# Gate and up tiles of three feed-forward stages as 2x2 block products with seven multiplications in place of eight

## The chip, the cores and the metric

The kernel runs as one program on one core of a Trainium2 chip. The metric is the device time of one execution in microseconds; the median of the runs shown stands for the kernel. A profiled execution gives the trace, from which all durations here are read. Engines: PE is TensorE (matrix products), PEld its weight loads, DVE is VectorE, ACT is ScalarE, POOL is GpSimd, SP issues the DMAs.

## What is computed

Two layers of feed-forward, token mixing, feed-forward, for 512 positions of width 1024, hidden width 2816, all in f32:

```python
def modulate(h, shift, scale):
    return h * (1 + scale) + shift

def swiglu(h, wi, wo):
    gate, up = jnp.split(h @ wi, 2, axis=-1)
    return (jax.nn.silu(gate) * up) @ wo
...
    for l in range(DEPTH):
        mod = (c_act @ ada_w[l] + ada_b[l]).reshape(b, N_MOD, 1, D_MODEL)
        ...
        h = modulate(rmsnorm(x, norm_ffn1[l]), sh1, sc1)
        x = x + 0.5 * g1 * swiglu(h, ffn1_wi[l], ffn1_wo[l])
        h = modulate(rmsnorm(x, norm_mix[l]), sh2, sc2)
        x = x + g2 * token_mixing(h, cos, sin, w_in[l], sink[l], onorm_a[l], onorm_b[l], w_out[l])
        h = modulate(rmsnorm(x, norm_ffn2[l]), sh3, sc3)
        x = x + 0.5 * g3 * swiglu(h, ffn2_wi[l], ffn2_wo[l])
    return rmsnorm(x, final_norm)
```

## The kernel before

Activations lie transposed: 8 tiles of 128 features by 512 positions. Every f32 operand is split into a high part that TensorE takes in one pass (type F32R) and a low rest, and a product is three matmuls: high by high, low weight by high, high weight by low (`mm3`, lines 153 to 155). The weights come from HBM as raw f32 pieces of 128x1024 and are split on the chip by `emit_chunk`: ScalarE copies the high part (line 134), VectorE subtracts it (line 135). Buffers: two for `raw`, six each for `hi` and `lo`; `ahead` keeps three pieces emitted beyond the one in use.

A feed-forward stage (`ffn`) works in three parts of 7, 7 and 8 hidden tiles (THIRDS). For each hidden tile there are a gate tile and an up tile, each 8 x 3 matmuls of 512 columns into one PSUM bank; `take` then makes the product: Silu on ScalarE (line 362), times up on VectorE (363), and the split into `gh` and `gl` (367, 368). At the end of a part `out_tiles` multiplies these by the second weight, 8 output tiles of 7 or 8 x 3 matmuls, and adds the result to x (line 306). The first four tiles of a stage (`group`) are computed in two halves of 256 positions, since the normalised input of the second half is not there yet: `Norm.make` (lines 221 to 224) writes it in `hh` and `hl`, from a row statistic that comes by way of `stat` and `bcast`. The last four output tiles of a stage are done in halves as well.

There are four such stages: layer 0 first and second, layer 1 first and second; the first is started in another way (`start`). Between them lie the two mixers. Beside all this VectorE makes the modulation vectors: `ada_col` loads a piece of `ada_w` and multiplies it by `cs` with a sum (line 240), a step after each tile of the first stage (56 columns after the first 16) and of layer 0's second feed-forward stage (72 columns, with `cs` made anew by `ada_open`, matmuls of line 271).

The order of instructions on each engine is set by a scheduler from the program's order, priorities and buffer releases; each engine then runs its own queue strictly in that order. Pools decide how far anything can run ahead.

## Time and profile before

| | us |
|---|---|
| median of three runs | 1985.97 (1984.81 to 1990.3) |
| profiled execution, own time | 1988.23 |
| its span | 1986.2 |
| PE busy in it | 1955.2 (98%) |
| DVE busy | 1171.7 (59%) |
| ACT busy | 751.0 (38%) |
| granted TensorE clock, mean | 0.995 |

Busy time is the sum of an engine's instruction intervals; the intervals of matmuls overlap, so the pace of TensorE is read from the starts of its instructions. The same holds on VectorE: an instruction may start while the one before it is still listed.

### The profile page before, as it was taken

The page shows a single profiled execution, that of the slowest core. Times are in us where ns is not written, and L with a number is a line of the kernel's source. Part 1 is how long each engine was busy: PE and PEld are TensorE (multiplying, and loading weights), DVE is VectorE, ACT ScalarE, POOL GpSimd, SP SyncE. Part 2 cuts the span into 40 slices and gives each one's busy share as a digit, 9 for nine tenths or more (in the row PEclk, how much of TensorE's full clock was granted, in tenths as well). Part 3 has the DMA queues.
Part 4 walks back from the last instruction along what each step waited for, and adds up shares of the span by engine and source line. Part 5 has one row for each costly group of instructions (what it writes and reads, how often), then busy time and mean ns, then how long its engine had stood idle before and what let it go on. Part 6 is the DMA issues. An engine that isn't in the chain of part 4 may idle for free.

```text
span 1986.2 us, 25905 instructions
## 1 busy us (share of the span) xinstructions
PE 1955.2 (98%) x10016; PEld 1655.4 (83%) x10016; DVE 1171.7 (59%) x2131; ACT 751.0 (38%) x1332; POOL 92.7 (5%) x69
## 2 busy tenths in 40 slices
PE   6999999999999999999999999999999999999998
PEld 5888888998778888888898888889877898888888
DVE  7988433576798898733463333337678983333333
ACT  4422222345685422222242222223556752222223
POOL 4000000011210000000000000000121000000000
PEclk8999999999999999999999999999999999999999
DMA  7789433234412698733332333331544123333331
GB/s 255 272 309 337 129 101 101 84 108 118 127 44 94 222 335 322 248 105 98 94 96 85 106 90 102 97 104 58 155 107 106 54 75 98 104 98 95 104 96 43
DMA packets 84941, 266.96 MB, mean 134 GB/s; under 512 B 10706, under 2 KB 13906, under 8 KB 84820
## 3 DMA queue, kind: packets, MB, share of 16 engines
q1 hardware_dynamic: 84820, 265.33, 41.7%
q8 instruction: 78, 1.28, 0.3%
q14 instruction: 43, 0.35, 0.1%
HBM read 244.31 MB, written 2.10 MB: 124 GB/s over the span
## 4 chain that ended last, share of the span: by engine, by line
PE 89%; DVE 4%; DMA 2%; issue 2%; ACT 1%; POOL 0%; SPq 0%; DVEq 0%; ACTq 0%; POOLq 0%
PE mm L155 26%; PE mm L153 26%; PE mm L154 26%; PE ptr L516 2%; PE po L523 1%; PE po L524 1%; PE s L486 1%; PE s L487 1%; DVE lo L135 1%; PE mm L455 1%; PE mm L457 1%; PE mm L456 1%; PE p L531 1%; DVE araw L240 1%; DMA raw<-in_wo_dram 0%
## 5 line engine op out<-in xcount | busy, mean ns | idle before, releaser
L153 PE MATMUL mm<-hh,hi 128*128 128x512 f32 (+1 forms) x1776 | 662.3, 374 | 7.7 <-ACT hh L223 7.7
L155 PE MATMUL mm<-hl,hi 128*128 128x512 f32 (+1 forms) x1776 | 659.4, 373 | 2.0 <-DVE hl L224 2.0
L154 PE MATMUL mm<-hh,lo 128*128 128x512 f32 (+1 forms) x1776 | 661.4, 373 | 0.0
L134 ACT ACTIVATE hi<-raw 128x1024 fp32r<-128x1024 f32 (+5 forms) x365 | 335.0, 927 | 662.4 <-PE mm L155 575.1
L135 DVE TENSOR_TENSOR lo<-raw,hi 128x1024 fp32r<-128x1024 f32 (+5 forms) x365 | 397.1, 1094 | 311.4 <-ACT hi L134 309.1
L153 PEld LDWEIGHTS mm<-hh,hi 128*128 128x128 f32 x1776 | 336.2, 189 | 66.4 <-ACT hh L223 9.4
L155 PEld LDWEIGHTS mm<-hl,hi 128*128 128x128 f32 x1776 | 335.6, 189 | 60.6 <-DVE hl L224 3.2
L154 PEld LDWEIGHTS mm<-hh,lo 128*128 128x128 f32 x1776 | 335.9, 189 | 56.9
L154 PE MATMUL mm<-gh,lo 128*128 128x512 f32 (+1 forms) x832 | 296.9, 357 | 0.0
L155 PE MATMUL mm<-gl,hi 128*128 128x512 f32 (+1 forms) x832 | 296.6, 356 | 0.2 <-DVE gl L368 0.2
L153 PE MATMUL mm<-gh,hi 128*128 128x512 f32 (+1 forms) x832 | 296.7, 357 | 0.0
L306 DVE SCALAR_TENSOR_TENSOR x<-mm,fin,x 128x512 f32<-128x512 f32 (+1 forms) x156 | 101.9, 654 | 196.3 <-PE mm L155 195.7
L240 DVE CUSTOM_DVE_ANT_0 araw<-araw,cs 128x1024 f32<-128x1024 f32 x136 | 166.7, 1237 | 26.9 <-DMA araw<-in_adaT_dram 26.1
L155 PEld LDWEIGHTS mm<-gl,hi 128*128 128x128 f32 x832 | 157.2, 189 | 23.1 <-DVE gl L368 0.6
L154 PEld LDWEIGHTS mm<-gh,lo 128*128 128x128 f32 x832 | 157.2, 189 | 22.6
L153 PEld LDWEIGHTS mm<-gh,hi 128*128 128x128 f32 x832 | 157.2, 189 | 22.5
L362 ACT ACTIVATE sg<-mm 128x512 f32<-128x512 f32 x88 | 52.5, 598 | 283.7 <-PE mm L155 281.3
L363 DVE TENSOR_TENSOR sg<-sg,mm 128x512 f32<-128x512 f32 x88 | 60.4, 687 | 158.9 <-PE mm L155 157.4
L408 POOL TENSOR_TENSOR part<-part,rs 128x512 f32<-128x512 f32 x26 | 34.5, 1326 | 1274.2 <-DVE part L406 1272.0
L495 ACT ACTIVATE sm<-sm,nb 128x512 f32<-128x512 f32 (+2 forms) x128 | 81.6, 638 | 30.8 <-DVE nb L491 30.8
L516 PE MATMUL ptr<-ident,sm 128*128 128x128 f32 x416 | 81.5, 274 | 0.9 <-DVE pl L520 0.9
L520 DVE TENSOR_TENSOR pl<-ptr,ph 128x512 fp32r<-128x512 f32 (+2 forms) x128 | 73.2, 584 | 8.4 <-ACT ph L519 7.4
(142 smaller groups left out, 1793.2 us busy)
## 6 DMA issues: line engine op xcount, KB each, us to landing
raw<-in_wi_dram SPq DMA_DIRECT2D x170, 512.0 KB, 3.5
araw<-in_adaT_dram SPq DMA_DIRECT2D x144, 512.0 KB, 5.4
raw<-in_wo_dram SPq DMA_DIRECT2D x64, 448.0 KB, 3.4
raw<-in_wo_dram SPq DMA_DIRECT2D x32, 512.0 KB, 3.5
raw<-in_wqk_dram SPq DMA_DIRECT2D x26, 512.0 KB, 3.5
raw<-in_w_out_dram SPq DMA_DIRECT2D x16, 512.0 KB, 3.5
kh<-qh SPq DMA_DIRECT2D x40, 128.0 KB, 2.3
kl<-t SPq DMA_DIRECT2D x40, 128.0 KB, 2.3
```

Source lines behind the costliest of these rows:

```text
L134: A.activation(hi[:, sl], raw[:, sl], AF.Copy)
L135: V.tensor_tensor(lo[:, sl], raw[:, sl], hi.bitcast(F32)[:, sl], op=ALU.subtract)
L153: T.matmul(ps, wh, X[0][:, s], start=start, stop=False)
L154: T.matmul(ps, wl, X[0][:, s], start=False, stop=False)
L155: T.matmul(ps, wh, X[1][:, s], start=False, stop=stop)
L240: return V.tensor_tensor_reduce(out=raw, in0=raw, in1=ada["cs"], scale=1.0, scalar=0.0, op0=ALU.mult, op1=ALU.add, accum_out=mod[:, l, ch, ...
L306: V.scalar_tensor_tensor(x[:, m, s], ps[:, s], gate[:, m:m + 1], x[:, m, s], op0=ALU.mult, op1=ALU.add)
L362: A.activation(sg, pg, AF.Silu)
L363: V.tensor_tensor(sg, sg, pu, op=ALU.mult)
L495: A.activation(s[:, :w], s[:, :w], AF.Exp, scale=-1.0, bias=self.nb[:, qt:qt + 1], accum_out=self.den[:, qt:qt + 1])
L516: T.transpose(p[:, j * 128:j * 128 + 128], self.sm[qt][:, c0:c0 + 128], ident)
L520: V.tensor_tensor(pl[:, :w], p[:, :w], ph.bitcast(F32)[:, :w], op=ALU.subtract)
```

## The change

In three of the four feed-forward stages (all but the first) the gate and up tile of one hidden tile become one 2x2 block product. Rows of blocks are the two halves of the positions (256 each), columns are gate and up, and the inner dimension of 1024 is cut in two halves of 4 feature tiles. Seven products, each 4 x 3 matmuls of 256 columns, replace the eight blocks that 48 matmuls of 512 columns stand for. The first three hidden tiles of a stage (PLAIN) stay as they were; 19 tiles in each of the three stages are done in the new way (`pair`).

The seven products need sums of blocks. Those of the activations are made once in a stage (`sums`: four tiles of 4x256, split in `sh`, `sl`). Those of the weights are made for each hidden tile on the chip (`emit_pair`): from the raw gate and up pieces VectorE makes five 512-column differences and sums (lines 180, 182, 187, 189 and the split of the fourth), and three and a half pieces are split into high and low in place of two. The results lie in two PSUM banks whose halves are used by turns; ScalarE copies three intermediate halves out (lines 479, 487, 490) and VectorE adds them (493, 496, 498), Silu works in place (499), and the product and its split are taken one tile later (506 to 510).

With it go changes of buffers and order: `raw` has four buffers; `cs` is kept, so the second `ada_open` is gone; the 72 columns of layer 1 are spread over three stages (16 in the first, 32 in layer 0's second, 24 in layer 1's first), there with one `araw` buffer; the mask table is loaded at the start of each mixer in place of once; a reserved scratch area in SBUF is made smaller.

```diff
+    def emit_pair():
...
+        rg, ru = (wp.tile([128, 1024], F32, tag="raw", name="raw", bufs=4) for _ in range(2))
+        for r, ap in zip((rg, ru), specs[i]):
+            nc.sync.dma_start(r, ap)
+        hs = [wp.tile([128, 1024], F32R, tag="hi", name="hi") for _ in range(3)]
+        ls = [wp.tile([128, 1024], F32R, tag="lo", name="lo") for _ in range(3)]
+        ta = pool.tile([128, 1024], F32, tag="ta", name="ta")
+        h4 = pool.tile([128, 512], F32R, tag="h4", name="h4")
+        l4 = pool.tile([128, 512], F32R, tag="l4", name="l4")
...
+        high(hs[0], rg)
+        V.tensor_tensor(t1, b12, b11, op=ALU.subtract)
+        yield
+        V.tensor_tensor(t2, t1, b22, op=ALU.subtract)
+        yield
+        low(ls[0], rg, hs[0])
+        yield
+        high(hs[1], ta)
+        V.tensor_tensor(b21, b21, t2, op=ALU.add)
+        A.activation(h4, b21, AF.Copy)
+        V.tensor_tensor(b12, b22, b12, op=ALU.subtract)
+        low(ls[1], ta, hs[1])
+        yield
+        high(hs[2], ru)
+        low(l4, b21, h4)
+        yield
+        low(ls[2], ru, hs[2])
...
+            def prod(ps, W, w0, X, start=False, stop=False):
+                for k in range(4):
+                    (wh, wl), (xh, xl) = (w[:, w0 + k * 128:w0 + k * 128 + 128] for w in W), X(k)
+                    T.matmul(ps, wh, xh, start=start and k == 0, stop=False, skip_group_check=True)
+                    T.matmul(ps, wl, xh, start=False, stop=False, skip_group_check=True)
+                    T.matmul(ps, wh, xl, start=False, stop=stop and k == 3, skip_group_check=True)
...
+            prod(bl, cA, 512, A_(4, HALF[0]), start=True, stop=True)
...
+            prod(a, cA, 0, A_(0, HALF[0]), stop=True)
+            A.activation(sc[:, 0], a, AF.Copy)
...
+            prod(c, cT, 0, S_(0), start=True, stop=True)
+            prod(br, c4, 0, A_(4, HALF[1]), stop=True)
+            A.activation(sc[:, 1:3], b2.rearrange("p (j n) -> p j n", n=HS), AF.Copy)
...
+            prod(a, cT, 512, S_(1), stop=True)
+            A.activation(sc[:, 3], a, AF.Copy)
...
+            prod(c, cD, 512, S_(3), stop=True)
+            V.tensor_tensor(up[:, HALF[0]], c, sc[:, 3], op=ALU.add)
+            prod(a, cD, 0, S_(2), stop=True)
+            sg = pool.tile([128, S], F32, tag="sg", name="sg", bufs=2)
+            V.tensor_tensor(sg.rearrange("p (j n) -> p j n", n=HS), b1.rearrange("p (j n) -> p j n", n=HS),
+                            sc[:, 0:2], op=ALU.add)
+            V.tensor_tensor(up[:, HALF[1]], a, sc[:, 2], op=ALU.add)
+            A.activation(sg, sg, AF.Silu)
...
-        raw = wp.tile([128, 1024], F32, tag="raw", name="raw", bufs=2)
+        raw = wp.tile([128, 1024], F32, tag="raw", name="raw", bufs=4)
...
+        mask = pool.tile([128, 896 + 384], F32, name="mask")
+        nc.sync.dma_start(mask, masks)
```

TensorE, last part of layer 1's first feed-forward stage, before: the end of one gate tile and the start of its up tile (`hh`, `hl` are the activations, `hi`, `lo` the weights).

```order
L154 MATMUL mm_10569<-hh7_8690,lo_10496 128x512
L155 MATMUL mm_10569<-hl7_8691,hi_10495 128x512
L153 MATMUL mm_10607<-hh0_8676,hi_10533 128x512 [waits Activation_49]
L154 MATMUL mm_10607<-hh0_8676,lo_10534 128x512
L155 MATMUL mm_10607<-hl0_8677,hi_10533 128x512
```

The same place after: the first matmul of six of a pair's seven products (`mm_12498` and `mm_12499` are its two banks, `sh` a sum of activations).

```order
L457 MATMUL mm_12498<-hh4_9773,hi_12389 128x256 [waits DVE_49]
...
L457 MATMUL mm_12498<-hh0_9765,hi_12389 128x256
...
L457 MATMUL mm_12499<-sh_10091,hi_12390 128x256 [waits DVE_49]
...
L457 MATMUL mm_12498<-sh_10091,hi_12390 128x256 [waits Activation_49]
...
L457 MATMUL mm_12499<-sh_10091,hi_12391 128x256 [waits Activation_49]
...
L457 MATMUL mm_12498<-sh_10091,hi_12391 128x256 [waits Activation_49]
```

Two tiles of 24 matmuls each became one run of 84 of half the width; a bank is written, copied out by ScalarE, and written again. In the whole program the matmuls of 512 columns fall from 6596 to 3858 and those of 256 rise from 2144 to 6932.

VectorE, the same place, before: all that it does for one hidden tile.

```order
L363 TENSOR_TENSOR sg_10594<-sg_10594,mm_10569 128x512 [waits PE_49]
L135 TENSOR_TENSOR lo_10703<-raw_10701,hi_10702 128x1024 [waits DMAHW3_49,Activation_49]
L368 TENSOR_TENSOR gl2_10598<-sg_10594,gh2_10597 128x512 [waits Activation_49]
L135 TENSOR_TENSOR lo_10741<-raw_10739,hi_10740 128x1024 [waits DMAHW4_49,PE_49,Activation_49]
```

After, for one hidden tile (`ta`, `raw` and `l4` are sums of weights; the row behind these is `up` of the next tile, line 493).

```order
L496 TENSOR_TENSOR sg_12492<-mm_12369,sc_12371 128x512 [waits PE_49]
L498 TENSOR_TENSOR up_12372<-mm_12369,sc_12371 128x256
L180 TENSOR_TENSOR ta_12653<-raw_12644,raw_12643 128x512 [waits DMAHW7_49,DMAHW0_49,DVE_49]
L506 TENSOR_TENSOR sg_12492<-sg_12492,up_12372 128x512 [waits DVE_49,Activation_49]
L177 TENSOR_TENSOR lo_12523<-raw_12515,hi_12520 128x1024
L510 TENSOR_TENSOR gl1_12497<-sg_12492,gh1_12496 128x512 [waits Activation_49]
L182 TENSOR_TENSOR ta_12653<-ta_12653,raw_12644 128x512
L177 TENSOR_TENSOR lo_12650<-raw_12643,hi_12647 128x1024 [waits PE_49,Activation_49]
L189 TENSOR_TENSOR raw_12644<-raw_12644 128x512
L177 TENSOR_TENSOR l4_12526<-raw_12514,h4_12525 128x512 [waits Activation_49]
L187 TENSOR_TENSOR raw_12643<-raw_12643,ta_12653 128x512 [waits DVE_49]
L177 TENSOR_TENSOR lo_12651<-ta_12653,hi_12648 128x1024 [waits PE_49,Activation_49]
```

Four rows became thirteen; the weights that are made here belong to the tile after the next one. In eleven of the 57 pairs a row of line 302 (a modulation column, 240 before) stands among them.

ScalarE, the same place, before.

```order
L362 ACTIVATE sg_10663<-mm_10607 128x512 [waits PE_49,Activation_49]
L134 ACTIVATE hi_10740<-raw_10739 128x1024 [waits DMAHW4_49]
L134 ACTIVATE hi_10771<-raw_10770 128x1024 [waits DMAHW5_49,PE_49]
L367 ACTIVATE gh3_10666<-sg_10663 128x512 [waits DVE_49]
```

After, for one hidden tile (`sc` are the copies out of PSUM).

```order
L499 ACTIVATE sg_12492<-sg_12492 128x512 [waits DVE_49]
L507 ACTIVATE gh1_12496<-sg_12492 128x512 [waits DVE_49]
L479 ACTIVATE sc_12500<-mm_12498 128x256 [waits PE_49,Activation_49]
L174 ACTIVATE hi_12647<-raw_12643 128x512 [waits DMAHW7_49]
L174 ACTIVATE hi_12647<-raw_12643 128x512
L188 ACTIVATE h4_12525<-raw_12514 128x512 [waits PE_49]
L487 ACTIVATE sc_12500<-mm_12499 128x512
L490 ACTIVATE sc_12500<-mm_12498 128x256 [waits PE_49]
L174 ACTIVATE hi_12648<-ta_12653 128x512
L174 ACTIVATE hi_12648<-ta_12653 128x512 [waits DVE_49]
L174 ACTIVATE hi_12649<-raw_12644 128x512 [waits DMAHW0_49,DVE_49,PE_49]
L174 ACTIVATE hi_12649<-raw_12644 128x512
```

Of the three copies the last (line 490) stands right behind `h4` and the copy of line 487, and ahead of four conversions; both `h4` and 487 wait for the fourth product.

## Rows read from the trace of the kernel before

**Rows 1.** The page, busy time: engine, us (share of the span), instructions.

```profile
PE 1955.2 (98%) x10016; PEld 1655.4 (83%) x10016; DVE 1171.7 (59%) x2131; ACT 751.0 (38%) x1332; POOL 92.7 (5%) x69
```

**Rows 2.** Windows: 512-column tiles, 256-column tiles, and two stretches of the first stage.

```profile
core 0: us, PE busy (x) PEld busy (x) DVE busy (x) ACT busy (x) POOL busy (x), PEclk, DMA share, GB/s
1700.00:1750.00 50.00, 50.00 (x223) 41.38 (x222) 18.67 (x19) 11.99 (x13) 0.00 (x0) 1.00 0.33 102
1347.00:1358.00 11.00, 11.00 (x94) 11.00 (x93) 4.82 (x10) 2.13 (x5) 0.00 (x0) 1.00 0.15 48
100.00:200.00 100.00, 99.84 (x441) 82.37 (x440) 85.42 (x132) 28.42 (x33) 0.00 (x0) 1.00 0.89 325
200.00:300.00 100.00, 100.00 (x443) 82.84 (x442) 41.51 (x50) 26.50 (x32) 0.00 (x0) 1.00 0.37 112
```

**Rows 3.** Timeline of PE, 512-column matmuls: start us, us, engine line op.

```profile
1700.09 0.39 PE L153 MATMUL mm<-gh,hi 128*128 128x512 f32 x1
...
1705.53 0.39 PE L153 MATMUL mm<-gh,hi 128*128 128x512 f32 x1
```

**Rows 4.** Timeline of PE, 256-column matmuls.

```profile
1347.03 0.28 PE L153 MATMUL mm<-gh,hi 128*128 128x256 f32 x1
...
1357.11 0.28 PE L153 MATMUL mm<-gh,hi 128*128 128x256 f32 x1
```

**Rows 5.** Lines by form: xcount, busy us, mean ns of one, idle before and releaser.

```profile
L153 PEld LDWEIGHTS mm<-gh,hi 128*128 128x128 f32 x832 | 157.2, 189 | 22.5
L135 DVE TENSOR_TENSOR lo<-raw,hi 128x1024 fp32r<-128x1024 f32 x203 | 258.4, 1273 | 234.7 <-ACT hi L134 232.7 <-issue 1.7
L240 DVE CUSTOM_DVE_ANT_0 araw<-araw,cs 128x1024 f32<-128x1024 f32 x136 | 166.7, 1237 | 26.9 <-DMA araw<-in_adaT_dram 26.1
L363 DVE TENSOR_TENSOR sg<-sg,mm 128x512 f32<-128x512 f32 x88 | 60.4, 687 | 158.9 <-PE mm L155 157.4 <-ACT sg L362 1.4
L534 DVE TENSOR_TENSOR o<-p,o 128x256 f32<-128x256 f32 x16 | 6.7, 417 | 1.0 <-ACT o L533 1.0
L367 ACT ACTIVATE gh<-sg 128x512 fp32r<-128x512 f32 x88 | 54.4, 618 | 18.3 <-DVE sg L363 17.8
L533 ACT ACTIVATE o<-p 128x256 f32<-128x256 f32 x16 | 6.0, 378 | 0.5 <-PE p L531 0.5
```

**Rows 6.** Timeline of DVE, four instructions with nothing between them.

```profile
1024.75 1.23 DVE L135 TENSOR_TENSOR lo<-raw,hi 128x1024 fp32r<-128x1024 f32 x1 [1.71 <-ACT hi L134]
1025.89 0.68 DVE L363 TENSOR_TENSOR sg<-sg,mm 128x512 f32<-128x512 f32 x1
1026.49 1.22 DVE L135 TENSOR_TENSOR lo<-raw,hi 128x1024 fp32r<-128x1024 f32 x1
1027.62 0.68 DVE L368 TENSOR_TENSOR gl<-sg,gh 128x512 fp32r<-128x512 f32 x1
```

**Rows 7.** Timeline of DVE, second half's input at a stage's start, first and last.

```profile
1015.52 0.87 DVE L221 SCALAR_TENSOR_TENSOR t<-x,fin,pR 128x256 f32<-128x256 f32 x2 [0.80 <-PE pR L209]
...
1022.15 0.89 DVE L224 SCALAR_TENSOR_TENSOR hl<-t,fin,hh 128x256 fp32r<-128x256 f32 x2 [0.19 <-ACT hh L223]
```

**Rows 8.** Timeline of PE: end of that group, and the matmuls of line 271.

```profile
1030.41 0.40 PE L153 MATMUL mm<-hh,hi 128*128 128x512 f32 x1
...
670.57 1.98 PE L271 MATMUL pc<-cr,orow 1*128 1x512 f32 x4
```

**Rows 9.** DMA issues: xcount, KB each, median us to landing; and the first use of the mask.

```profile
raw<-in_wi_dram SPq DMA_DIRECT2D x170, 512.0 KB, 3.5
araw<-in_adaT_dram SPq DMA_DIRECT2D x144, 512.0 KB, 5.4
mask<-in_masks_dram SPq DMA_DIRECT2D x1, 640.0 KB, 6.6
...
418.08 0.33 SPq L130 DMA_DIRECT2D raw<-in_wv_dram  x1
434.43 0.69 DVE L491 CUSTOM_DVE_ANT_0 sm<-s,mask 128x512 f32<-128x512 f32 x1 [1.88 <-PE s L487]
```

More of the change, by code (lines that the diff above doesn't have):

```diff
@@ L23 @@
 THIRDS = ((0, 7), (7, 7), (14, 8))
+PLAIN = 3
 EPS = 1e-6
@@ L85, in tile_trunk @@
     fin = const.tile([128, L, 9, KD], F32, name="fin")
-    mask = const.tile([128, 896 + 384], F32, name="mask")
+    cs = const.tile([128, 1024], F32, name="cs")
     rc = const.tile([128, S], F32, name="rc")
@@ L90, in tile_trunk, with paired @@
     nsnk = const.tile([128, L * 8], F32, name="nsnk")
+    def paired(l, sub, f):
+        return l + sub > 0 and f >= PLAIN
+    temps = [None, None]
     specs = []
@@ L123, in emit_chunk @@
             return
+        if isinstance(specs[i], tuple):
+            for _ in emit_pair():
+                pass
+            return
         state["emit"] += 1
@@ L136, in emit_chunk, with parts, high, low @@
         live[i] = (hi, lo)
+    def parts(t):
+        return [t[:, a:a + 512] for a in (0, 512)]
+    def emit_pair():
+        i = state["emit"]
+        state["emit"] += 1
+        pool = temps[0]
+        rg, ru = (wp.tile([128, 1024], F32, tag="raw", name="raw", bufs=4) for _ in range(2))
[6 more added lines that the diff above has]
+        l4 = pool.tile([128, 512], F32R, tag="l4", name="l4")
+        live[i] = (*zip(hs, ls), (h4, l4))
+        b11, b21 = parts(rg)
+        b12, b22 = parts(ru)
+        t1, t2 = parts(ta)
+        def high(dst, src):
+            for d, r in zip(parts(dst), parts(src)):
+                A.activation(d, r, AF.Copy)
+        def low(dst, src, h):
+            V.tensor_tensor(dst, src, h.bitcast(F32), op=ALU.subtract)
+        high(hs[0], rg)
[15 more added lines that the diff above has]
+        low(ls[2], ru, hs[2])
     LA = 3
@@ L147, in ahead @@
     def ahead(n=LA):
-        while state["emit"] < min(state["use"] + n, len(specs)):
+        while state["emit"] < len(specs):
+            due = sum(3 if isinstance(specs[i], tuple) else 1 for i in range(state["use"], state["emit"]))
+            if due > 1 if isinstance(specs[state["emit"]], tuple) else due >= n:
+                return
             emit_chunk()
@@ L349, in ffn @@
         temps[:] = pool, "sg"
+        wino = l + sub > 0
+        Sx = []
+        if wino:
+            norm.t = [pool.tile([128, S], F32, tag=f"g{'hl'[k % 2]}{4 + k // 2}", name="t") for k in range(KD)]
+            for k in range(norm.made):
+                hh, hl = norm.h[k]
+                V.scalar_tensor_tensor(norm.t[k][:, HALF[0]], hh.bitcast(F32)[:, HALF[0]], sh[:, k:k + 1],
+                                       hl.bitcast(F32)[:, HALF[0]], op0=ALU.subtract, op1=ALU.add)
+            both = tiny.tile([128, 4], F32, tag="both", name="both", bufs=1)
+            V.tensor_tensor(both, sh[:, 0:4], sh[:, 4:8], op=ALU.add)
@@ L373, in ffn @@
                 for p in (start() if start else group(norm, gs, sh, 4)):
+                    if wino:
+                        sums(done)
                     take(p)
@@ L377, in ffn @@
                         step()
-            for _ in range(done, 2 * n):
+            flat = 2 * min(n, max(0, PLAIN - f0)) if wino else 2 * n
+            for _ in range(done, flat):
                 W = chunk()
@@ L384, in ffn @@
                 ahead()
-                step()
+                if not wino:
+                    step()
+            wait = []
+            for _ in range(flat // 2, n):
+                wait += pair(g, wait)
+            for last in wait:
+                last()
             if ti == 2:
@@ L771, in tile_trunk @@
     ada_list += [(0, ch, k) for ch in range(2, 9) for k in range(KD)]
+    ada_list += [(1, ch, k) for ch in range(2) for k in range(KD)]
     def rope_tables():
@@ L799, in step0 @@
         ada_step()
-        if not tables[0] and len(ada_list) < 48:
+        if not tables[0] and len(ada_list) < 64:
             tables[0] = True
```

113 lines of the change are left out of this document (83 added, 30 removed).

## The prediction

> **What bounds the kernel now.** I read the busy shares first: TensorE 98%, VectorE 59%, ScalarE 38% of a span of 1986.2 us [rows 1]. Then the windows: in tiles of 512 columns and in tiles of 256 columns TensorE is busy all the time, at a granted clock of 1.00, which is the 2.4 GHz level, while VectorE has 37% and 44% [rows 2]. So a feed-forward stage lasts as long as its matmuls, and what the change is worth is the pace of TensorE's two kinds of matmul. That is read from starts, not from durations, since matmuls overlap: 24 matmuls of 512 columns take 1705.53 - 1700.09 = 5.44 us, 0.2267 us each [rows 3]; 84 of 256 columns take 1357.11 - 1347.03 = 10.08 us, 0.1200 us each [rows 4]. Half the width costs 53% of the time, and this decides how much of one product in eight is left.
>
> **The change: TensorE.** Before, one hidden tile's gate and up are 48 x 0.2267 = 10.88 us. After, they are 84 x 0.1200 = 10.08 us, and 84 is just the stretch that rows 4 span. Saved: 0.80 us a pair, 57 pairs, 45.6 us. The second making of `cs` goes, and with it 1.98 us of TensorE [rows 8]. Together 47.6 us, all on the bounding engine.
>
> The Trainium skill's page "TensorE: Matmul & The Clock Gate" (Back-to-back issue gap) puts the gap of matmuls in a row at columns/2.4 plus 2.5 ns. The trace disagrees, with 226.7 and 120.0 ns against 215.7 and 109.2 by the Trainium skill [rows 3, 4]. By the Trainium skill, as an estimate, a pair would save 1.18 us and the change 67 us before its costs. The measurement decides, and the sum above rests on it alone.
>
> **VectorE in a pair.** It now has thirteen rows a pair in place of four: three splits of 1024 columns, five operations of 512 on weights, three of 512 on results, two of 256. By mean durations (1.273, 0.687, 0.417) [rows 5] that is 3.82 + 5.50 + 0.83 = 10.15 us. In a run without waits, though, starts follow at 1.14 for 1024 and 0.60 for 512 columns [rows 6], some 0.08 less than a duration; by that the pair costs 3.42 + 4.80 + 0.68 = 8.9 us. The price lies between 8.9 and 10.15 against TensorE's 10.08. I take the lower end, since rows 6 are of just these forms back to back, but VectorE goes from 44% to about 90%. In eleven pairs a modulation column is added, 1.15 by the same reckoning, so 10.0: even. VectorE runs nearly a tile ahead with weights, so a lag of 3 us in a few pairs reaches nothing. Cost in a steady pair: nothing; cover gone, whatever exceeds 10.08 is paid in full.
>
> **ScalarE in a pair.** Ten operations of 512 columns at 0.618 and two copies of 256 at 0.378 [rows 5]: 6.9 of 10.08 us. What matters is one copy: TensorE may not overwrite a bank half for the seventh product before ScalarE has copied it out (line 490). It has the sixth product to do so, 12 x 0.12 = 1.44 us. In the steady order `h4` and the copy of line 487 stand ahead of it; both can start after the fourth product and take 0.62 + 0.62, less than the fifth product's 1.44. So the copy starts when the fifth product ends and is done 0.38 later, 1.06 to spare. Cost nothing.
>
> **Stage starts.** Here VectorE is crowded. The 16 rows of the second half's input end near 1023.0 [rows 7]. Behind them, up to `l4` of the first pair, the order has twelve operations of 256 at 0.40 (a pair of them shows 0.87), four of 256 at 0.34, four splits of 1024 for the sums of activations at 1.14, seven of 512 for the plain tiles, and the first pair's weights, five of 512 and three of 1024: 4.8 + 1.4 + 4.6 + 4.2 + 3.0 + 3.4 = 21.4, so 1044.4. TensorE ends the group at 1030.4 [rows 8], does two plain tiles (10.9) and needs `l4` 36 matmuls later, at 1045.6: in time by 1.2 us. But in this first pair the copy of line 490 stands behind the `h4` of the second pair, and so behind 4.7 us more of VectorE: 1049.1 + 0.62 + 0.38 = 1050.1 against the 1049.9 at which TensorE wants the half. Each hand-over between engines adds 0.19 [rows 7]. A stall of 0 to 4 us; I take 1.5, for some eight hand-overs on that way, times three stages: 4.5 us.
>
> **Ends of parts.** After a part's last pair the first output tile needs `gl` of that pair: sum 0.69, up 0.34, Silu 0.62, product 0.69, `gh` 0.62, `gl` 0.69, and five hand-overs of 0.19, so 4.6 us, up to 1.1 more where a wo piece or a modulation column is queued between. TensorE has 20 other matmuls first, 4.5 us. 0 to 1.1 us, nearer the lower end, 0.3; nine parts: 2.7 us.
>
> **Moved transfers.** A pair loads 1 MB in 10 us, where SP's loads of 512 KB land in 3.5 [rows 9]. The modulation columns now have one buffer, so their load waits in SP's queue for VectorE, and weight loads wait behind it; in the eleven pairs three loads follow one another, and a piece can come 0 to 1 us late. The lag above covers that; I take 0.8 us in all. The 16 columns moved into the first stage cost 16 x 1.24 = 20 us of VectorE and 8 MB; there DMA is at 0.89 and TensorE at 99.8% in 100 to 200 us, but in the next hundred DMA is at 0.37 and VectorE at 42% [rows 2], which hides them. The mask load lands in 6.6 us; it now stands behind a load issued at 418.1, and the first use is at 434.4 [rows 9]: hidden; uncovered, 6.6 us twice. More `raw` buffers only let loads start earlier. The smaller scratch area is not in use by any queue that I see; nothing.
>
> **Sum.** 1986.2 - 47.6 + 4.5 + 2.7 + 0.8 = 1946.6 us span. The profiled execution's own time is 1988.23, the median of the runs 1985.97, that is 2.3 lower, so 1948.6 becomes **1946** for the median. Bounds: no stall at all gives 1938; all stalls at their upper ends (12, 10 and 2) give 1962.
>
> **Rivals.** *VectorE becomes the bound of the pair.* For it: even at 8.9 it is at 88%, and five of its rows wait for ScalarE, with 0.19 us of idle time at such a hand-over [rows 7]. If half of these land in its queue, a pair takes its durations' 10.15 plus 0.4, or 10.5, and the eleven with a column 11.7: 0.42 x 46 + 1.6 x 11 = 37 more than the 1938, so 1975; if rows 6 hold and only waits come on top, about 1958. Middle 1966. Against: the durations overlap in rows 6, and most results from ScalarE are ready long before.
>
> *The copy out of the shared half bounds the pair (slower than before).* If ScalarE's conversions stand ahead of line 490 not only in a stage's first pair but in effect in all, because ScalarE is late, the copy ends two conversions, `h4` and itself after the fifth product: 3 x 0.62 + 0.38 + 0.19 on either side = 2.6 against 1.44 of cover, 1.2 us of stall a pair. 57 x 1.2 = 68 us takes the gain and 20 more: 1938 + 68 = 2006. It decides from 47.6 / 57 = 0.84 us a pair. Against: in the order the four conversions stand behind the copy, and ScalarE has 3 us free in a pair.
>
> *Weight loads bound TensorE.* A pair has 84 loads in place of 48, a load lasts 189 ns [rows 5], and in the 256-column stretch the load queue is busy all the time [rows 2]. One after another they would take 84 x 0.189 = 15.9 us a pair, 5.0 more than before, 2270 in all. Against it stand the starts 0.12 us apart with a load for each [rows 4]: loads overlap. The Trainium skill's page "Perfetto Trace Analysis" (Identifying the Most-Contended Engine) wants TensorE judged by the busy share of LDWEIGHTS rather than of matmuls, and by that rule this change makes the worse share worse. The trace shows the share at 100% and the pace kept.
>
> **How the numbers follow.** Forecast (TensorE bounds, 1938 to 1962): 0.77. VectorE bounds: 0.17. Copy bounds: 0.05. Loads bound: 0.01. A measurement of this kernel can tell about 0.3%, 6 us, from no change. Faster: the forecast and nine tenths of the VectorE case, 0.92; within: the rest of that case and a little of the copy's, 0.03; slower: the other two, 0.05. The range of 8 in 10 goes from 1938, the sum without stalls, to 1966, the middle of the VectorE case.
>
> **What would show it.** Right: matmuls of the pairs 0.12 us apart from first to last, 10.1 us from one pair's first matmul to the next's, idle time of TensorE only in the first pair of a stage and at the first output tile of a part; VectorE near 90% in the pairs. Wrong: a pair at 10.5 or more with TensorE waiting for a low part of weights (VectorE) or for line 490 (the copy); matmul starts that are not 0.12 apart with three operands from sums; a clock under 1.00 in the pairs; idle time in the mixers, which I left as they were.

## The result, and the profile after

The changed kernel takes **1954.17 us** (median of 4 runs, 1951.09 to 1955.42) where the kernel before, run beside it, takes 1987.85: 33.7 us less, a ratio of 0.9829 with the 95% interval 0.9808 to 0.985. Forecast were 1946 and 40 us less. The time lies inside the range, and the gain is 6 us short of the forecast.

The page after: busy shares, the chain that ended last (by engine, then by line), two groups of instructions, and the loads of the modulation columns.

```profile
PE 1915.1 (98%) x12064; PEld 1718.1 (88%) x12064; DVE 1510.1 (77%) x2713; ACT 939.2 (48%) x1798; POOL 94.9 (5%) x69
...
PE 77%; DMA 9%; DVE 8%; issue 3%; ACT 2%; SPq 1%; POOL 0%; DVEq 0%; ACTq 0%; POOLq 0%
PE mm L217 14%; PE mm L216 14%; PE mm L215 14%; PE mm L457 9%; PE mm L458 8%; PE mm L459 8%; DMA araw<-in_adaT_dram 8%; DVE araw L302 3%; PE ptr L685 2%; DVE lo L147 1%; PE po L692 1%; PE po L693 1%; PE s L655 1%; PE s L656 1%; PE mm L624 1%
...
L215 PE MATMUL mm<-gh,hi 128*128 128x512 f32 (+1 forms) x832 | 298.2, 358 | 5.5 <-ACT gh L507 5.5
...
L302 DVE CUSTOM_DVE_ANT_0 araw<-araw,cs 128x1024 f32<-128x1024 f32 x136 | 167.7, 1236 | 57.9 <-DMA araw<-in_adaT_dram 57.5
...
araw<-in_adaT_dram SPq DMA_DIRECT2D x144, 512.0 KB, 4.6
```

TensorE is at 98%, as before [rows 1], and that share tells nothing. The chain tells more: 8% of the span, 156 us, stands on loads of one tensor, `araw`, and VectorE's 26.1 us of waiting for them [rows 5] have become 57.5. Of these 40.6 lie in the two stages whose columns now have one buffer, the rest in the first stage.

Where the gain arose is seen by stages, each from the last output matmul of one stage to the last of the next:

| stage (us) | before | after | modulation columns in it, after |
|---|---|---|---|
| layer 0, first feed-forward | 398.0 | 397.4 | 88 |
| layer 0, second | 365.3 | 354.6 | 32 |
| layer 1, first | 363.3 | 358.1 | 24 |
| layer 1, second | 363.7 | 349.2 | none |

The two mixers took 243.2 and 242.6 us before and 242.1 and 241.8 after. The last three rows are the stages with pairs, called first, second and third below. The stage without columns gained 14.4 us, close to 19 x 0.80 = 15.2. The two with columns gained 10.7 (2 of it the second `cs`) and 5.2. So the block product pays, and something in two stages takes some 15 us back.

The pairs' pace, two matmuls of TensorE's timeline that are 84 starts apart, in the third stage:

```profile
1753.73 0.28 PE L458 MATMUL mm<-sh,lo 128*128 128x256 f32 x1
...
1763.83 0.28 PE L458 MATMUL mm<-sh,lo 128*128 128x256 f32 x1
```

10.10 us a pair. Windows of the second stage (its second part, then three stretches at that part's end), and of the same stage's third part, for comparison, where no column stands among the pairs:

```profile
core 0: us, PE busy (x) PEld busy (x) DVE busy (x) ACT busy (x) POOL busy (x), PEclk, DMA share, GB/s
1108.00:1182.00 74.00, 71.42 (x588) 70.75 (x587) 66.27 (x100) 41.22 (x76) 0.00 (x0) 1.00 0.56 178
1176.00:1182.00 6.00, 6.00 (x52) 6.00 (x52) 4.24 (x6) 3.79 (x7) 0.00 (x0) 1.00 0.87 243
...
1186.00:1189.50 3.50, 0.70 (x4) 0.24 (x2) 3.50 (x6) 1.24 (x2) 0.00 (x0) 1.00 0.88 273
1189.50:1194.00 4.50, 4.30 (x11) 3.18 (x12) 2.99 (x6) 0.98 (x2) 0.00 (x0) 0.64 0.74 252
...
1225.00:1306.00 81.00, 81.00 (x672) 80.82 (x672) 64.67 (x90) 47.24 (x88) 0.00 (x0) 1.00 0.37 118
```

Behind 1186 TensorE stands, and then goes on at a mean granted clock of 0.64. What it stands for is read backwards, from TensorE's, ScalarE's, VectorE's and SP's timelines in turn (an idle time and its releaser in brackets):

```profile
1186.31 0.39 PE L217 MATMUL mm<-gl,hi 128*128 128x512 f32 x1
1189.58 0.50 PE L215 MATMUL mm<-gh,hi 128*128 128x512 f32 x1 [2.87 <-ACT gh L507]
```

```profile
1186.96 0.63 ACT L499 ACTIVATE sg<-sg 128x512 f32<-128x512 f32 x1 [3.38 <-DVE sg L496]
1188.89 0.63 ACT L507 ACTIVATE gh<-sg 128x512 fp32r<-128x512 f32 x1 [1.30 <-DVE sg L506]
```

```profile
1178.55 0.08 DVE L302 DVE_READ_ACCUMULATOR2_ANT mod<- 128x1 f32 x1
...
1183.76 1.22 DVE L302 CUSTOM_DVE_ANT_0 araw<-araw,cs 128x1024 f32<-128x1024 f32 x1 [3.52 <-DMA araw<-in_adaT_dram]
...
1184.91 0.42 DVE L493 TENSOR_TENSOR up<-mm,sc 128x256 f32<-128x256 f32 x1
...
1186.25 0.68 DVE L496 TENSOR_TENSOR sg<-mm,sc 128x512 f32<-128x512 f32 x1
```

```profile
1178.66 0.33 SPq L297 DMA_DIRECT2D araw<-in_adaT_dram  x1
```

The previous column frees `araw` at 1178.6, SP issues the next load then (the last line), and VectorE can start on it 5.1 us later, at a DMA share of 0.87. VectorE has long arrived at that column and stands 3.52 us, with the last pair's sums behind it in its queue. They come late, so does `gh`, and the first output tile waits 2.87 us. In the two stages with columns TensorE has two more idle times of over 0.4 us:

```profile
831.66 0.50 PE L215 MATMUL mm<-gh,hi 128*128 128x512 f32 x1 [2.29 <-ACT gh L507]
1126.71 0.39 PE L457 MATMUL mm<-sh,hi 128*128 128x256 f32 x1 [2.23 <-ACT sc L479]
```

The first is another end of a part. The second lies inside a pair: there a column was waited for 1.99 us, the sum behind it came late, and with it Silu and `gh` on ScalarE, behind which the copy of line 479 is queued. The clock's share shows in TensorE's timeline behind the stall at 1189.6, and where it is over:

```profile
1191.21 0.63 PE L216 MATMUL mm<-gh,lo 128*128 128x512 f32 x1
1191.63 0.63 PE L217 MATMUL mm<-gl,hi 128*128 128x512 f32 x1
...
1194.42 0.40 PE L215 MATMUL mm<-gh,hi 128*128 128x512 f32 x1
1194.65 0.40 PE L216 MATMUL mm<-gh,lo 128*128 128x512 f32 x1
```

0.42 us from start to start in place of 0.23, the lower of the two clock levels (1.2 GHz); 4.5 us at a mean of 0.64 cost another 1.6. Together the two stages have 9.1 us of idle time and 3.4 us of the clock, out of roughly 15 us. The Trainium skill's page "TensorE: Matmul & The Clock Gate" (Architectural detail, the paragraph on engine queue depths) calls VectorE's and ScalarE's queues strictly first in, first out. The trace agrees: `up` and `sg` were ready and did not pass the column.

### The profile page after: what moved, and what is told of

Read it like the earlier page. It is cut to its first block, busy times and chain, and to the rows that moved or that the text cites. A ratio compares the mean times of both kernels' runs of the same rounds, so it can differ in the third digit from the quotient of the medians.

```text
span 1953.6 us, 31187 instructions
## 1 busy us (share of the span) xinstructions
PE 1915.1 (98%) x12064; PEld 1718.1 (88%) x12064; DVE 1510.1 (77%) x2713; ACT 939.2 (48%) x1798; POOL 94.9 (5%) x69
## 4 chain that ended last, share of the span: by engine, by line
PE 77%; DMA 9%; DVE 8%; issue 3%; ACT 2%; SPq 1%; POOL 0%; DVEq 0%; ACTq 0%; POOLq 0%
PE mm L217 14%; PE mm L216 14%; PE mm L215 14%; PE mm L457 9%; PE mm L458 8%; PE mm L459 8%; DMA araw<-in_adaT_dram 8%; DVE araw L302 3%; PE ptr L685 2%; DVE lo L147 1%; PE po L692 1%; PE po L693 1%; PE s L655 1%; PE s L656 1%; PE mm L624 1%
## 5 line engine op out<-in xcount | busy, mean ns | idle before, releaser
L215 PE MATMUL mm<-hh,hi 128*128 128x512 f32 (+1 forms) x864 | 307.2, 357 | 7.4 <-ACT hh L286 6.8
L217 PE MATMUL mm<-hl,hi 128*128 128x512 f32 (+1 forms) x864 | 304.4, 357 | 2.7 <-DVE hl L287 2.7
L216 PE MATMUL mm<-hh,lo 128*128 128x512 f32 (+1 forms) x864 | 306.3, 356 | 0.0
L457 PE MATMUL mm<-sh,hi 128*128 128x256 f32 x912 | 260.4, 286 | 3.3 <-ACT sc L479 2.6
L458 PE MATMUL mm<-sh,lo 128*128 128x256 f32 x912 | 258.0, 283 | 0.0
L459 PE MATMUL mm<-sl,hi 128*128 128x256 f32 x912 | 257.9, 283 | 0.0
L302 DVE CUSTOM_DVE_ANT_0 araw<-araw,cs 128x1024 f32<-128x1024 f32 x136 | 167.7, 1236 | 57.9 <-DMA araw<-in_adaT_dram 57.5
L215 PEld LDWEIGHTS mm<-hh,hi 128*128 128x128 f32 x864 | 164.6, 191 | 29.9 <-ACT hh L286 8.1
L217 PEld LDWEIGHTS mm<-hl,hi 128*128 128x128 f32 x864 | 164.1, 191 | 25.7 <-DVE hl L287 4.0
L457 PEld LDWEIGHTS mm<-sh,hi 128*128 128x128 f32 x912 | 174.1, 191 | 4.6 <-ACT sc L479 3.0
L458 PEld LDWEIGHTS mm<-sh,lo 128*128 128x128 f32 x912 | 174.3, 191 | 0.0
```

Of the source, the lines that this page charges most:

```text
L215: T.matmul(ps, wh, X[0][:, s], start=start, stop=False)
L216: T.matmul(ps, wl, X[0][:, s], start=False, stop=False)
L217: T.matmul(ps, wh, X[1][:, s], start=False, stop=stop)
L302: return V.tensor_tensor_reduce(out=raw, in0=raw, in1=cs, scale=1.0, scalar=0.0, op0=ALU.mult, op1=ALU.add, accum_out=mod[:, l, ch, k:k + ...
L457: T.matmul(ps, wh, xh, start=start and k == 0, stop=False, skip_group_check=True)
L458: T.matmul(ps, wl, xh, start=False, stop=False, skip_group_check=True)
```

## Experiments on the columns

**Theory W**: the wait for the one buffer. **Rivals**: V, VectorE's work on the columns, and D, their transfers' bandwidth.

There is no room in SBUF for a second `araw` tile, but the tile `st` is free once a stage's sums are made.

```diff
-        raw = home.tile([128, 1024], F32, tag="araw", name="araw", bufs=n)
+        ada["turn"] = turn = ada.get("turn", 0) + 1
+        if n == 1 and turn % 2:
+            raw = home.tile([128, 4, HS], F32, tag="st", name="araw").rearrange("p j n -> p (j n)")
+        else:
+            raw = home.tile([128, 1024], F32, tag="araw", name="araw", bufs=n)
```

> The changed kernel with one edit: in the two stages with modulation columns the columns alternate between the buffer araw and the tile st, which nothing uses after a stage's start. VectorE's work on the columns and their 56 transfers stay. Theory W (VectorE stands in its queue, up to 3.5 us at a time, until the next column has landed in the one buffer; the pairs' sums behind it come late, TensorE idles 2.2 to 2.9 us and then runs at a lower granted clock): the wait of VectorE for the columns' loads falls from 57.5 us to under 15, the stages with columns fall from 354.6 and 358.1 us to about 349 each, and the time from 1954.2 to 1939 us (1937 to 1943). Theory V (the columns' 1.2 us of VectorE's work each, in pairs that leave VectorE no room for it): no change, 1952 to 1956. Theory D (the columns' transfers take bandwidth from the weights'): no change, 1952 to 1956.

Measured: 1947.73 us (1943.86 to 1950.1), the two stages 352.2 and 351.1. The direction is W's, the size is not: VectorE's wait fell to 29.0 us, not under 15, and 9.4 of the roughly 15 us in these stages were back, 6.4 us in the median (the profiled execution also has a first stage of 402.0 us, which the edit doesn't touch). 22 columns still stand among pairs (24 in the changed kernel), and of the 29.0 us of waiting 10.4 are in these stages. Three views of this kernel, VectorE's at the end of a part, ScalarE's and TensorE's, show that a short wait and a column together are enough:

```profile
831.28 1.23 DVE L306 CUSTOM_DVE_ANT_0 araw<-araw,cs 128x1024 f32<-128x1024 f32 x1 [0.27 <-DMA araw<-in_adaT_dram]
...
832.43 0.69 DVE L500 TENSOR_TENSOR sg<-mm,sc 128x512 f32<-128x512 f32 x1
```

```profile
833.15 0.63 ACT L503 ACTIVATE sg<-sg 128x512 f32<-128x512 f32 x1 [2.32 <-DVE sg L500]
```

```profile
835.76 0.50 PE L215 MATMUL mm<-gh,hi 128*128 128x512 f32 x1 [1.37 <-ACT gh L511]
```

Between W, V and D this left things open. So the load went and the work stayed:

```diff
-        nc.sync.dma_start(raw, adaT[l, ch * KD + k])
+        late = n == 1
+        if not late:
+            nc.sync.dma_start(raw, adaT[l, ch * KD + k])
...
-        return V.tensor_tensor_reduce(out=raw, in0=raw, in1=cs, scale=1.0, scalar=0.0, op0=ALU.mult,
+        return V.tensor_tensor_reduce(out=raw, in0=cs if late else raw, in1=cs, scale=1.0, scalar=0.0, op0=ALU.mult,
```

> The changed kernel without the 56 loads of modulation columns in the two stages that carry them; VectorE still does its 1.2 us for each, on data that is there, so the modulation values of the second layer are not computed. Theory W (wait for the one buffer's load): 1937 to 1943 us, the two stages at about 349 us. Theory V (VectorE's work on the columns): 1952 to 1956. Theory D (the loads' bandwidth): 1937 to 1943. Together with the kernel with two buffers it tells W (both fast) from D (only this one fast) and V (both slow).

Measured: 1941.28 us (1940.56 to 1941.67), the stages 348.9 and 348.7. 23 columns still stand among pairs and cost nothing: V falls.

Then all columns into the first stage:

```diff
-    ada_list += [(1, ch, k) for ch in range(2) for k in range(KD)]
+    ada_list += [(1, ch, k) for ch in range(9) for k in range(KD)]
...
-        ada_step()
-        if not tables[0] and len(ada_list) < 64:
+        for _ in range(2):
+            ada_step()
+        if not tables[0] and len(ada_list) < 120:
```

> The changed kernel with the 56 modulation columns of the second layer all done in the first stage, two at a step, so that no stage with pairs has a column. All three theories say that the two stages then take about 349 us, as the third one did. What it tells apart is the price in the first stage: it moves 28 MB more, and at the 397 us it now takes the share of its transfers rises. If its tiles stay bound by TensorE the time is 1937 to 1943 us; if the transfers or VectorE bound it, the first stage grows by 5 to 40 us and the time is 1945 to 1980.

Measured: 1948.13 us (1947.05 to 1950.27). The stages with pairs are at 348.8, 348.7 and 349.3; the first went from 397.4 to 405.0. About half of what was won there was paid here, 4.9 us of it in one idle time of TensorE for weights not yet split; that is the lower end of the second case.

Last, two buffers and another place: a column is queued behind the residual update of an output tile, one and two by turns.

```diff
+            for _ in range((2, 1)[ada["i"] % 2]):
+                with tc.issue_after(after):
+                    ada_step()
...
-                step()
+                step(done) if ada["pool"][1] == 1 else step()
```

> The kernel with two buffers (1947.7 us) with one more edit: VectorE's work on a column is queued behind the residual update of an output tile, one or two columns a tile, so that all 56 columns lie among the output tiles and none stands between the sums of a pair. The two stages took 352.2 and 351.1 us with two buffers, and 348.9 and 348.7 us without the loads. Theory W (only a wait for a column ahead of a pair's sums is felt; 10.4 us of such waits were left with two buffers): both stages at 349 to 350 us, no idle time of TensorE over 1 us in the second parts, 1938 to 1944 us. Theory O (what was left with two buffers is the columns' own VectorE work, wherever it lies, or their transfers): 351 to 352 us a stage, 1945 to 1950 us.

Measured: **1941.12 us** (1940.81 to 1943.16), ratio 0.9769 (0.9756 to 0.9783); stages 348.8, 348.7, 349.3. All 56 loads and all of their work are there. They have moved too, but the weights land no sooner for it (`raw` from `in_wi_dram` in a median of 3.4 us, 3.3 in the changed kernel), so D falls as well. The kernel's chain, and VectorE's wait for columns in the whole program:

```profile
PE 92%; DVE 3%; issue 1%; ACT 1%; DMA 1%; POOL 0%; SPq 0%; DVEq 0%; ACTq 0%; POOLq 0%
```

```profile
DVE araw L306 <- DMA araw<-in_adaT_dram: 16.0, 25, 1.3
```

Of the 16.0 us 11.7 lie in the first stage; in the two stages with columns the wait went from 40.6 us with one buffer to 10.4 with two and to 4.3 here. What is left stands among output tiles and reaches nobody: in both stages TensorE's timeline has no gap over 0.2 us. W holds, with the addition that the columns' place counts beside their buffers: the second buffer gave back 9.4 us of the two stages' lengths, the place behind it the other 5.8. The place alone, with one buffer, was not tried.

## Experiments on the rest of the sum

**The change without its pairs**, to price the block product alone:

```diff
-        return l + sub > 0 and f >= PLAIN
+        return False
...
-        wino = l + sub > 0
+        wino = False
```

> The changed kernel with the block products off in all three stages (ordinary tiles, eight multiplications), its other edits kept: one buffer for the columns, columns as the new order has them, no second silu of the conditioning. It prices the rest of the change alone. Theory W: the wait for a column reaches TensorE only where VectorE is three quarters busy, so here it costs nothing, and the time is that of the kernel before less 2 us: 1983 to 1987. If one buffer alone costs its 15 us without pairs too: 1996 to 2002.

Measured: 1996.35 us, 1.0041 (1.0028 to 1.0053) of the time before. By its number that is the second expectation, but not by its reason: the stages with columns are as long as the one without (365.8, 365.9, 366.3), so the buffer is not it. TensorE's timeline of this kernel, two matmuls 24 starts apart:

```profile
1834.64 0.40 PE L215 MATMUL mm<-gh,hi 128*128 128x512 f32 x1
...
1840.24 0.40 PE L215 MATMUL mm<-gh,hi 128*128 128x512 f32 x1
```

5.60 us where [rows 3] has 5.44, 0.2333 each, without an idle moment, in every stage, and in `gh` and `gl` alone (those of 256 columns that read `gh` and `gl` start 0.118 apart, a little sooner than 0.120). As built, these tiles begin 96 bytes past a multiple of 128 in SBUF; in the kernel before and the changed one they begin on such multiples. The missing tile of 16 bytes (`both`) does that.

```diff
         wino = False
+        both = tiny.tile([128, 4], F32, tag="both", name="both", bufs=1)
+        V.memset(both, 0.0)
```

> The kernel without pairs took 1996 us, 11 us over what was expected, without a new stall: its 432 matmuls of 512 columns in each stage that read the tiles gh and gl started 0.2333 us apart, against 0.2267 in the kernel before and in the changed kernel, and those that read hh and hl 0.2267 as ever. Without the small tile of the pairs the tiles gh and gl begin 32 bytes past a multiple of 64 in SBUF. Here the one edit is that small tile, 16 bytes a partition, allocated again (and set to zero) in every stage, which moves them back onto multiples of 64. Theory A (the place of the moving operand sets the 3%): 0.2267 us again, 4 x 432 x 0.0067 = 11.5 us less, 1983 to 1987 us. Theory B (something else of the kernel without pairs): 1994 to 1998 us.

Measured: 1985.67 us (1984.03 to 1986.84), 0.9989 (0.998 to 0.9998), the stages 363.1, 363.2, 363.7: theory A. The first of them is 2.2 us shorter than before, which is the second `cs`; the column buffer costs nothing here, though VectorE waits 59.9 us for columns in the two stages. Against it the kernel with late columns is 44.6 us faster, 0.78 a pair.

**How much room VectorE has.** Two, then four more operations of 1024 columns in each pair:

```diff
-            V.tensor_tensor(up[:, HALF[0]], c, sc[:, 3], op=ALU.add)
+            mark = V.tensor_tensor(up[:, HALF[0]], c, sc[:, 3], op=ALU.add).ins
+            with tc.issue_after(mark):
+                for _ in range(2):
+                    V.tensor_tensor(cs[:, :1024], cs[:, :1024], cs[:, :1024], op=ALU.max)
```

> The kernel with late columns with two more VectorE operations of 1024 columns in each pair, behind the first sum of the pair; their result changes nothing. VectorE is busy 45.4 of 50.5 us in five pairs of the third stage, 9.07 of 10.1 us a pair; each operation adds 1.14 by its starts, so a pair asks VectorE for 11.2 to 11.35 us. Theory of the prediction (VectorE's time counts from start to start, 8.9 us a pair, and it would bound the pairs from 10.1 on): 1.1 to 1.25 us more in each inner pair, some 48 of the 57, so 50 to 65 us over the kernel with late columns. If VectorE's order, not its sum, sets the end (the sums behind the added work come 2.3 us late in each pair and TensorE waits for them): over 100 us. If there is more room than that: under 20 us.

Measured: 1946.81 us, 5.7 more than with late columns; no expectation came out but the last. VectorE's timeline shows the first sum (`up`) of a part's last four pairs:

```profile
1859.93 0.41 DVE L504 TENSOR_TENSOR up<-mm,sc 128x256 f32<-128x256 f32 x1
...
1871.09 0.41 DVE L504 TENSOR_TENSOR up<-mm,sc 128x256 f32<-128x256 f32 x1
...
1882.24 0.42 DVE L504 TENSOR_TENSOR up<-mm,sc 128x256 f32<-128x256 f32 x1
...
1890.60 0.42 DVE L504 TENSOR_TENSOR up<-mm,sc 128x256 f32<-128x256 f32 x1
```

11.16 and 11.15 us from one to the next, then 8.36: VectorE falls behind and makes it up. It can, because the last pairs of a part have less to do (the weights they prepare are the output's): 10 operations stand between the last two sums, 15 between the others. So the sum over a part should decide. Windows of the kernel with late columns, the pairs of the third stage's three parts:

```profile
core 0: us, PE busy (x) PEld busy (x) DVE busy (x) ACT busy (x) POOL busy (x), PEclk, DMA share, GB/s
1611.60:1652.00 40.40, 40.40 (x330) 40.04 (x329) 36.47 (x50) 26.00 (x48) 0.00 (x0) 1.00 0.42 137
1690.30:1760.80 70.50, 70.50 (x581) 70.12 (x580) 55.40 (x77) 39.87 (x76) 0.00 (x0) 1.00 0.36 109
1799.10:1880.00 80.90, 80.90 (x667) 80.52 (x666) 65.15 (x90) 46.70 (x88) 0.00 (x0) 1.00 0.36 113
```

With two operations, 4, 7 and 8 pairs and 1.14 each, VectorE has 45.6, 71.4 and 83.4 us to do: 8.6 over in a stage, 26 in three, of which 20 vanish, some 2.2 us a part. With four, by the same account:

> The kernel with late columns with four more VectorE operations of 1024 columns in each pair in place of two. Two cost 5.7 us in all (1946.8 against 1941.1), although an inner pair then asked VectorE for 11.1 of TensorE's 10.1 us. Theory M (the mean over the pairs of a part decides, since the weights of two chunks ahead are a store: VectorE was busy 36.5, 55.4 and 65.2 us of the 40.4, 70.5 and 80.9 us of the three parts; four operations make that 54.7, 87.3 and 101.7, over by 52 us a stage, of which the store takes up some 2 us a part): 2060 to 2080 us. Theory F (VectorE's operations are cheaper beside these pairs than their starts say, and two did not fill it): under 1990 us.

Measured: 2064.1 us (2060.75 to 2064.89), 123 more than with late columns: theory M. TensorE's longest waits in this kernel (us in total, times, longest) are for the copy that is line 479 in the changed kernel and 490 here; it waits in its turn for VectorE's last sum of the pair before, which reads the same tile `sc`:

```profile
PE mm L468 <- ACT sc L490: 58.6, 31, 2.6
```

**How much room the copy out of the shared half has.** Three more ScalarE copies ahead of it:

```diff
+            mark = A.activation(sc[:, 1:3], b2.rearrange("p (j n) -> p j n", n=HS), AF.Copy).ins
+            with tc.issue_after(mark):
+                for _ in range(3):
+                    mark2 = A.activation(cs[:, :512], cs[:, :512], AF.Copy).ins
...
+            with tc.issue_after(mark2):
+                A.activation(sc[:, 3], a, AF.Copy)
```

> The kernel with late columns with three more ScalarE copies of 512 columns in each pair, queued between the copy of the shared half's bank and the next copy out of PSUM; their result changes nothing. They add 3 x 0.62 = 1.86 us a pair to ScalarE, which is busy 6.7 of 10.1. Theory of the prediction (the copy has 1.06 us to spare until the next product but one into its bank): 0.8 us more in each pair, 45 us over the kernel with late columns. If ScalarE evens it out over the pair (its order lets the copy go ahead of weight work that waits anyway): under 10 us.

Measured: 1956.93 us, 15.8 more, 0.28 a pair; between the two. The waits of TensorE that the trace names are not for this copy but for the one ahead of it (line 498 here, 487 in the changed kernel):

```profile
PE mm L468 <- ACT sc L498: 3.4, 5, 1.1
```

The starts of TensorE's timeline tell more. As means over the 57 pairs, against the kernel with late columns, the seventh product, which needs the copy in question, begins 0.13 us late, and the sixth, which needs the one ahead of it, 0.08. So 1.86 us of work in front of the copy cost it 0.13 a pair: as an estimate from these two numbers some 1.7 us were free, not 1.06.

**A stage's start.** One ordinary pair less:

```diff
-PLAIN = 3
+PLAIN = 2
```

> The kernel with late columns in which each of the three stages does 20 pairs as block products in place of 19: two ordinary pairs at a stage's start in place of three. Three more block pairs give 3 x 0.78 = 2.3 us. Theory S (a stage's start has room: no idle time of TensorE was seen there with three): 1938 to 1940 us. Rival: the first block pair needs the sums of the tile halves one ordinary pair, 10.9 us, earlier, VectorE and ScalarE are not done, and TensorE waits 2 to 6 us a stage: 1944 to 1957 us.

Measured: 1957.18 us, 16 more: the rival, at its upper end of 1957. TensorE's waits for the sums of activations in the whole program, then windows of the third stage's start:

```profile
PE mm L470 <- DVE sl L444: 5.4, 5, 1.3
PE mm L468 <- ACT sh L443: 4.1, 3, 1.4
```

```profile
core 0: us, PE busy (x) PEld busy (x) DVE busy (x) ACT busy (x) POOL busy (x), PEclk, DMA share, GB/s
...
1619.00:1624.00 5.00, 1.87 (x6) 1.29 (x7) 5.00 (x11) 2.63 (x4) 0.00 (x0) 0.85 0.00 0
1624.00:1630.00 6.00, 6.00 (x33) 6.00 (x31) 5.78 (x7) 2.66 (x5) 0.00 (x0) 0.56 0.02 4
```

9.5 us of waiting; of the other 8.9 (16.1, and the 2.3 that were to be won) most is the clock: 6 us at 0.56 are 2.6 us here, and over TensorE's busy time the granted clock costs the three stages 1.7, 3.0 and 3.1 us.

**The place of the operands**, on the kernel with late columns: first all tiles of a stage but `hh` and `hl` 32 bytes further, then the sums of activations.

```diff
+        off = tiny.tile([128, 4], F32, tag="off", name="off", bufs=1)
+        V.memset(off, 0.0)
```

> The kernel with late columns and one more tile of 16 bytes a partition ahead of each feed-forward stage's tiles, so that these begin 32 bytes past a multiple of 64; hh and hl stay where they were. Without pairs this cost 0.0067 us in each matmul of 512 columns that reads gh or gl, and nothing was seen in those of 256 columns. Theory A (the same here): 4 x 432 x 0.0067 = 11.5 us more, 1951 to 1954 us. If the 912 matmuls of 256 columns a stage that read the sums of halves, sh and sl, pay 0.0067 us too: some 18 us on top, 1968 to 1973 us. If the place matters only without pairs: 1940 to 1943 us.

Measured: 1942.37 us (1941.6 to 1942.71), as without; the theory in its form fell. That the time lies in the last range is no proof of its reason: two effects cancel. The matmuls of 512 columns that read `gh` did slow down to 0.2333 us. Those of 256 columns got faster; twelve starts of TensorE's timeline within a product:

```profile
1731.10 0.28 PE L471 MATMUL mm<-sh,lo 128*128 128x256 f32 x1
...
1732.50 0.28 PE L471 MATMUL mm<-sh,lo 128*128 128x256 f32 x1
```

1.40 us, 0.1167 each in place of 0.1200 (over all that read the sums, hand-overs between products included, 0.1187 in place of 0.1206). A product that reads `hh` and `hl`, which stayed, with the weights `h4` and `l4` (`h` and `l` in the trace), which moved, got faster as well; eleven starts:

```profile
1728.09 0.28 PE L470 MATMUL mm<-hh,h 128*128 128x256 f32 x1
...
1729.39 0.28 PE L472 MATMUL mm<-hl,h 128*128 128x256 f32 x1
```

1.30 us, 0.118 each. So the offset slows one kind of matmul and speeds up another, and the second can be had without the whole of the first:

```diff
+            for tag in ("off", "sh0", "sl0", "sh1", "sl1", "sh2", "sl2", "sh3", "sl3", "off2"):
+                pool.tile([128, 8] if tag[0] == "o" else [128, 4, HS], F32 if tag[0] == "o" else F32R, tag=tag, name=tag)
```

> The kernel with late columns, with the eight tiles sh and sl of the pairs' sums of halves alone beginning 32 bytes past a multiple of 64, and gh, gl, hh and hl on multiples of 64. With all of a stage's tiles moved by 32 bytes the time stayed (1942.4 against 1941.1) because two things cancelled: the 432 matmuls of 512 columns a stage that read gh and gl started 0.2333 us apart in place of 0.2267 (2.9 us a stage more), while the 912 of 256 columns that read sh and sl started 0.1187 apart on average in place of 0.1205 (1.6 us a stage less) and those of 256 columns that read gh, gl, hh and hl gained 1.4 more. Theory A (the offset itself does both): only the second is left here, 3 x 1.6 = 5 us less, 1935 to 1938 us. Theory B (the two hang together in another way): 1940 to 1943 us.

Measured: **1934.16 us** (1933.33 to 1936.63), ratio 0.9735 (0.9722 to 0.9748), stages 346.9, 346.8, 347.0: a little more than theory A's gain, and the fastest kernel of this study, 20 us under the changed one. It doesn't move the sums alone: in the three stages with pairs `gh`, `gl`, `h4` and `l4` begin 64 bytes past a multiple of 128, and the matmuls of 512 columns that read `gh` and `gl` lie between the other two:

```profile
1770.73 0.39 PE L216 MATMUL mm<-gh,lo 128*128 128x512 f32 x1
...
1772.79 0.39 PE L216 MATMUL mm<-gh,lo 128*128 128x512 f32 x1
```

Nine starts in 2.06 us, 0.229 each. So the 7 us are the sum of several moves; the sums' own part is not priced. A placement with `gh` and `gl` on multiples of 128 was not tried.

## Why the prediction was right, and where it was off

- **Pace and TensorE's sum: right.** 84 starts took 10.10 us where 10.08 was read from [rows 4], with four of seven products reading sums of activations and a bank used by turns. The pairs' own worth, 44.6 us against 45.6, is measured between two kernels that differ in the pairs and in the columns' place. The second `cs` gave 2.2 against 1.98 [rows 8].
- **Moved transfers: the step that failed.** The term was 0.8 us with bounds of 0 and 2. The one buffer was seen, and also that the load waits for VectorE; what was weighed was weight loads that wait behind it in SP's queue. Not weighed was VectorE itself, which waits for the landing (4.6 us in the median, 5.1 at the place shown) with a pair's sums behind it. Nor were there eleven columns among the pairs but 24, in 18 pairs. "A lag of 3 us in a few pairs reaches nothing" holds for weights, which are made nearly a tile ahead, and not for the sums, which are wanted at once at a part's end. Measured: 15.2 us in the two stages' lengths between the changed kernel and the one with late columns, 13.1 us between the medians. 3.4 us of it are the clock, which no term had.
- **Ends of parts: right without a column, too low with one.** In the stage without columns no end of a part stalls, against 0.3 forecast. A column queued between was priced at 1.1, its work; with its wait it cost 2.29 and 2.87 us of idle time at two ends, before the clock.
- **Stage starts: 4.5 forecast, nothing seen**, in any of the three. That the margin is small was right: with one ordinary pair less, a start stalls.
- **VectorE as the rival: not met.** 8.9 us a pair by starts was nearly right; in five inner pairs of the third stage of the kernel with late columns VectorE is busy 45.4 of 50.5 us, 9.1 a pair. "Whatever exceeds 10.08 is paid in full" was wrong: it is the sum over a part that has to exceed TensorE's, and two more operations a pair cost 5.7 us, not 50. So the 0.17 that this rival was given was high.
- **The copy as the rival: not met.** Its place was right and its slack undersized, 1.06 against some 1.7. Another copy, that of line 479, did hold TensorE once, for 2.23 us, behind a column that was waited for.
- **Weight loads as the rival: not met.** The load queue is busy 80.82 of 81.00 us in the pairs, 191 ns a load, and the pace of rows 4 was kept. That the loads don't set this pace either is seen where the operands moved: the same loads go at 0.1167. The Trainium skill's page "Perfetto Trace Analysis" (Identifying the Most-Contended Engine) takes this share, beside the share of peak FLOPs, as the measure of how far TensorE is from its limit; here it stood at its end before the limit was reached.

Together: 8 us of losses were forecast, spread over starts, ends and transfers; some 15 came, from one cause that stood among them with 0.8. That the time still came within 8 us of the forecast is in part luck: the 7.2 us forecast for starts and ends stood for stalls that were not seen without a column, and they cover half of the 15.

## What to carry to other kernels

When a load gets one buffer, ask who stands waiting for the landing in which in-order queue, and what is queued behind it; the landing time, not the work, is then the price, and if TensorE idles for it the clock can add to it. Off-path work that waits for a transfer belongs behind a point where its engine has nothing urgent, and a mark in the order gave back here what a second buffer had left. An engine close to full is judged by its sum over the stretch that its store of finished work covers, not by the busiest unit in it.

## What the hardware showed

- **The place of a matmul's operands in SBUF changes its pace, in both directions.** For F32R operands, with TensorE never idle at a granted clock of 1.00, by the place of the moving operand: on multiples of 128 bytes 0.2267 us for 512 columns and 0.1200 for 256; 32 bytes past, 0.2333 and 0.1167; 96 past, 0.2333 and 0.118; 64 past, 0.229 for 512. The weights' place counts too: 0.118 for 256 columns with only the weights 32 bytes past. The Trainium skill's page "SBUF — State Buffer" (Specifications) gives cachelines of 16 bytes; all these offsets are multiples of 16, so by that alone none of them should differ. What lies behind it no run here tells.
- **A short idle time can be followed by the lower clock, and need not be.** After 2.87 us of TensorE's idle time the mean granted clock was 0.64 over the next 4.5 us, and in the third stage's start with one ordinary pair less, where TensorE was busy 1.87 of 5 us, 0.56 over the next 6. So that stall of 2.87 us cost about 4.5. But after the 2.23 us at 1126.7 in the changed kernel the clock stayed at 1.00, and in the kernel with four more VectorE operations some idle times of 2.64 us were followed by 1.00 and others by the lower level. What decides it no run here tells.
